# First mixer of a hybrid backbone: gate products on quarters of the TensorE array, and ScalarE in order of issue

## Chip, cores and metric

The kernel runs on one core of one Trainium2 chip. The metric is the device time of one launch in microseconds, as the median of several runs. All inputs start in device memory, laid out by the host in the order in which the kernel loads them; the output is written back there. A core has five engines that matter here: TensorE (PE in the profile; PEld is its weight loads), VectorE (DVE), ScalarE (ACT), GpSimd (POOL) and SyncE (SP), whose queue issues the loads. Each engine takes its instructions one after another, and waits for the others by semaphores.

## The reference, cut to what matters

Two layers work on 256 context tokens and 256 latent tokens of width 1024. Each layer is a SwiGLU feed-forward block, a mixer and a second feed-forward block, with normalisation and modulation around each. The mixer projects to 18 groups of 128 columns, works on them in three families (an RG-LRU on 512 columns, a gated short convolution, a chunked spatial gate) and projects back. The change is about the RG-LRU, for 8 heads of 64 channels and two directions d:

```python
xc = dwconv(p0, lru_conv_w, lru_conv_b, left=2)          # 4 taps, 512 channels
xh = xc.reshape(B, L, 8, 64)
r = sigmoid(einsum('blhi,hij->blhj', xh, w_r[d]) + b_r[d])  # per head: 64 x 64
i = sigmoid(einsum('blhi,hij->blhj', xh, w_i[d]) + b_i[d])
log_a = -8 * r * softplus(-lam[d]);  a = exp(log_a)
bx = sqrt(-expm1(2 * log_a)) * (i * xc)
h = linear_scan(a, bx, h0)                                # h_t = a_t h_(t-1) + bx_t
o_lru = gelu(lru_gate) * (h_forward + h_backward)
```

The second direction runs over the flipped sequence. The latent scan starts from the last state of the context scan. The second layer needs the context only up to its scan states.

## The kernel before, in words

Channels lie on the 128 partitions, tokens on the free axis: context tokens in columns 0 to 255, latent tokens in 256 to 511. A large product is made three times, on the high parts and the low parts of its operands (mm3, col_mm): each weight tile is loaded as `raw`, ScalarE casts it to `hi` and VectorE subtracts to get `lo` (split, L173 and L174), in two halves of 512 columns. `load_split` has four raw buffers and six of hi and lo each. All matmuls pass through one helper, so that they show as line L113.

`mixer(0, ...)` first makes six groups of the input projection (`front`: the four groups of the RG-LRU's input and two of its gates), and then issues the parts named in ORDER[0]. A part is a letter and a number; the engine set in MANUAL, TensorE alone, takes its instructions in exactly this order, while the other engines are ordered by the scheduler. The parts are:

- c, x, b: the three products of the short convolution, 24 products of 512 columns each, with a ScalarE copy (c) or VectorE work behind them
- g, u: a product of 24 and a Gelu on ScalarE; v: four token tiles of 24 products with 256 columns, from two weight units (16 and 17), each holding half of the contraction; m: the spatial mixing, on tiles of 64 columns
- C: the convolution of the RG-LRU for one group c of 128 channels, one ScalarE operation (L701) and three on VectorE (L703)
- G: the gates of a group. Its weights `wbd` are a block diagonal of two heads, 128 x 128, for r and i and both directions, loaded by one DMA of 256 KB (L714). Four products in plain float32 follow, each with a PSUM bank of its own, four sigmoids (L719, L723), and a VectorE product
- D: exp and tanh (L730, L731) and three VectorE operations for each direction
- S: for each direction a root on ScalarE (L741), a VectorE product and the scan (L744, L747, L748), then the sum, the gate, and `put`, which casts the result to high and low parts for the output projection

Weights are fetched ahead in order of use. The function `unit` fills a queue up to three units, and takes the first; a fill issues a unit's DMA and its casts:

```python
def fill(n):
    while units and len(queue) < n:
        queue.append(units.pop(0)())

def unit(ahead=2):
    fill(ahead + 1)
    return queue.pop(0)
```

PSUM has six banks for such products (`pbank`). ScalarE's functions come from tables: a change between sigmoid, exp and tanh, root, and Gelu shows as an ACT_TABLE_LOAD in the trace. After ORDER[0] come the products of the output projection, which need the results 4 to 7 first and 0 to 3 after them. The second layer's mixer has an ORDER of its own; it makes no low parts for its output, and `put` only notes the tile there.

Of the kernel before, what the change touches and what calls it, by code (L numbers as in the profile page):

```python
# [34 lines left out]
PARK = {2: 2, 3: 3, 6: 0, 7: 1}  # L35
NTMP = 3
NSQ = 3
JACC = 'gvg'
FIRST = 2

LAG = ((2.25, 2.1, 1.5), (5.75, 3.75, 1.75))
MANUAL2 = {mybir.EngineType.PE, mybir.EngineType.DVE}
# [3 lines left out]

LATE = ((0,), (1, 2, 3))
MANUAL = {mybir.EngineType.PE}

ORDER = ("c1 C0 g3 G0 C1 C2 C3 D0 c0 x1 G1 G3 D3 x0 S0 D1 v0 S3 G2 b0 g2 D2 u0 m0 S1 b1 u1 m1 S2",  # L50
         "c0 x0 C1 C0 C3 C2 g3 g2 G1 G0 D1 D0 c1 b0 u0 v0 S1 w0 G3 u1 x1 b1 m1 w1 S0 m0 G2 w2 p1 w3 w4 w5 p2 p5 w6 D2 S2 w7 p0 "
         "D3 S3 p7 p4 p3 p6")

TAIL = 4

# [26 lines left out]
def backbone(ctx: ExitStack, tc: tile.TileContext, xT, vecs, crow, w_mod, w_in, w_out, w_mi, w_mo, w_lru, w_cm, b_cm, lam, w_last, out):  # L82
    nc = tc.nc
    ve, sc, gp, te = nc.vector, nc.scalar, nc.gpsimd, nc.tensor
# [3 lines left out]
    tp = ctx.enter_context(tc.tile_pool(name="tp", bufs=2))  # L88
# [7 lines left out]
    def nm(s):  # L96
        cnt[0] += 1
        return f"{s}_{cnt[0]}"

    def tt_(dt=F32, shape=(P, T)):  # L100
        return tp.tile(list(shape), dt, tag="t", name=nm("t"), bufs=NT)

    def pbank():
        return ps.tile([P, 512], F32, tag="mm", name=nm("mm"))
# [23 lines left out]
    pe = Products()  # L128
# [226 lines left out]
    class Norms:  # L355
# [28 lines left out]
        def add(self, s, m):  # L384
# [245 lines left out]
    def mixer(l, segs, nxt, plan, skew_out, order_of, next_unit=None):  # L630

        a0, b0 = SEGS[segs[0]][0], SEGS[segs[-1]][1]
# [8 lines left out]
        for c in range(4):  # L641
            t = tt_(shape=(P, 2, SEQ + 3))
# [54 lines left out]
        def conv(c):  # L697
            xc = tt_()
            o = xc.rearrange("p (s t) -> p s t", s=2)
            cw = lambda k: V("conv_w", (l * 4 + k) * 4 + c)  # L700
            sc.activation(o, xp[c][:, :, 0:SEQ], AF.Identity, scale=cw(0), bias=V("conv_b", l * 4 + c))  # L701
            for k in range(1, 4):
                ve.scalar_tensor_tensor(o, xp[c][:, :, k:k + SEQ], cw(k), o, op0=OP.mult, op1=OP.add)  # L703
            return xc

        xcs, rs, ix, es = {}, {}, {}, {}
        heads = [(c, d, (l * 2 + d) * 4 + c) for c in range(4) for d in range(2)]

        def lru_conv(c):
            xcs[c] = conv(c)  # L710

        def lru_gates(c):
            wbd = tp.tile([P, 4, P], F32, tag="wbd", name=nm("wbd"))
            nc.sync.dma_start(wbd, w_lru[l, c])  # L714
            for c, d, b in heads[2 * c:2 * c + 2]:
                pr = pbank()
                pe.matmul(pr, lhsT=wbd[:, 2 * d, :], rhs=xcs[c], start=True, stop=True)
                r = rs[c, d] = tt_()
                sc.activation(r, pr, AF.Sigmoid, bias=V("b_r", b))  # L719
                pi = pbank()  # L720
                pe.matmul(pi, lhsT=wbd[:, 2 * d + 1, :], rhs=xcs[c], start=True, stop=True)
                i = ix[c, d] = tt_()
                sc.activation(i, pi, AF.Sigmoid, bias=V("b_i", b))  # L723
                ve.tensor_tensor(i, i, xcs[c], op=OP.mult)

        def lru_decay(c):
            for c, d, b in heads[2 * c:2 * c + 2]:
# [7 lines left out]
                ve.tensor_scalar(e, e, -1.0, 1.0, op0=OP.mult, op1=OP.add)  # L735
                es[c, d] = e

        def lru_scan(c):
            for c, d, _ in heads[2 * c:2 * c + 2]:
                e, h, b = es[c, d], rs[c, d], ix[c, d]  # L740
                sc.activation(h, h, AF.Sqrt, scale=-1.0)  # L741
                ve.tensor_tensor(b, b, h, op=OP.mult)
                if d == 0:
                    ve.tensor_tensor_scan(h, e, b, 0.0, op0=OP.mult, op1=OP.add)  # L744
                else:
                    r1, r2 = slice(SEQ - 1, None, -1), slice(T - 1, SEQ - 1, -1)
                    ve.tensor_tensor_scan(h[:, r1], e[:, r1], b[:, r1], 0.0, op0=OP.mult, op1=OP.add)  # L747
                    ve.tensor_tensor_scan(h[:, r2], e[:, r2], b[:, r2], h[:, 0:1], op0=OP.mult, op1=OP.add)  # L748
            h = rs[c, 1]
            ve.tensor_tensor(h[:, a0:b0], h[:, a0:b0], rs[c, 0][:, a0:b0], op=OP.add)  # L750
            ve.tensor_tensor(h[:, a0:b0], h[:, a0:b0], gates[c][:, a0:b0], op=OP.mult)
            put(c, h)

        sc_o, sc_p = {}, {}

# [32 lines left out]
        def chunk_v():  # L788
            wv = [unit(), unit()]
            for tt in range(a0 // P, b0 // P):  # L790
                tok = slice(tt * P, tt * P + P)
                p = pbank()
                mm3(p[:, :256], lambda k: hh[:, k, tok], lambda k: hl[:, k, tok],
                    lambda k: wv[k // 4][0][:, k % 4, :], lambda k: wv[k // 4][1][:, k % 4, :], range(KT))
                if tt % 2 == 0:
                    vt = tt_()
                vs[tt] = vt[:, (tt % 2) * 256:(tt % 2) * 256 + 256]
                sc.activation(vs[tt], p[:, :256], AF.Gelu_apprx_tanh)
# [34 lines left out]
        def out_mm(m, ks):  # L833
            i, o = OUT_AT[m]
            for k in ks:
                first = i not in banks
                if first:
                    banks[i] = pbank()
                pe.matmul(out_bank(m), lhsT=wo[m][:, k, :], rhs=oh[k][:, a0:b0], start=first,
                          stop=(k == LATE[1][-1] and (m + 1 == KT or OUT_AT[m + 1][0] > i)))  # L840

        def out_part(k):
            for m in range(KT):
                out_mm(m, (k,))

        parts = dict(w=out_load, p=lambda m: out_mm(m, (4, 5, 6, 7)), g=gate, c=short_c, x=short_x, b=short_b, v=lambda _: chunk_v(), u=chunk_u, m=chunk_mix,
                     C=lru_conv, G=lru_gates, D=lru_decay, S=lru_scan)
        def issue():
            for part in order_of.split():
                parts[part[0]](int(part[1]))  # L850

        if len(segs) == 2:
            with tc.manual_schedule(engines=MANUAL):
                issue()
            norms = Norms(segs, None, l, 1, nxt)
            order = [4, 5, 6, 7, 0, 1, 2, 3]
            y = norms.y = [tt_() for _ in range(KT)]

            def load(m):
                hi, lo = unit()  # L860
                return (lambda k: hi[:, order[k], :]), (lambda k: lo[:, order[k], :])

            out_phase(range(KT), load, [oh[k] for k in order], [ol[k] for k in order], y, KT,
                      ranges(segs, skew_out), norms.on_y, 0, 1)
            return
# [5 lines left out]
        need(l, 8)  # L871
        need(nxt[0], 3 * nxt[1])
        need(nxt[0], 3 * nxt[1] + 1)
        with tc.manual_schedule(engines=MANUAL):
            issue()
            for k in LATE[0]:
                out_part(k)
        with tc.manual_schedule(engines=MANUAL2):
            pieces = unit_pieces(next_unit)
            yg = [tt_() for _ in range(KT // 2)]  # L880
            acc = [tt_() for _ in range(2)]
# [280 lines left out]
    def keep_up(n):  # L1162

        p = pbank()
        for _ in range(n):
# [5 lines left out]
    ffn(0, 0, both, (0, 1, both), first_units, SKEW)  # L1171

    mixer(0, both, (0, 2, both), staged, SKEW, ORDER[0])
    ffn(0, 1, both, (1, 0, both), staged, SKEW)
    ffn(1, 0, both, (1, 1, both), staged, SKEW, turn=True)
    mixer(1, lat, (1, 2, lat), staged[2:] + staged[:1], 0, ORDER[1],
          lambda j: w_in[1, 1, j])
# [73 lines left out]
```

## Time and profile before

| | |
|---|---|
| median of 3 runs | 1646.99 us (1646.67 to 1647.06) |
| the profiled execution | 1642.21 us, of it 1640.4 us span |
| TensorE busy | 1612.5 us, 98% of the span |
| VectorE, ScalarE, GpSimd busy | 1164.3, 736.7, 120.3 us |
| mean granted clock of TensorE | 0.997 |

The time is that of the launch on the device; the span goes from the first to the last instruction of the profiled execution. An engine's busy time counts the time in which it ran instructions; waiting isn't in it. Matmuls are pipelined, so that one lasts longer in the records than its distance to the next.

### The profile page before, as it was taken

To read this page: it belongs to the slowest core of one execution; us is meant where nothing else is said; L and a number is where in the kernel's file an instruction comes from. 1 tells how busy PE (TensorE), PEld (TensorE's weight loads), DVE (VectorE), ACT (ScalarE), POOL (GpSimd) and SP (SyncE) were. 2 spreads that over 40 slices of the span, in tenths; PEclk is the share of its full clock that TensorE was granted. 3 is DMA by queue.
4 is the path that set the end of the run, shared out by engine and by line. 5 is a ranking of instruction groups with operands and counts; after the bars stand their busy time and mean duration, and the time that the engine had idled before them with its cause. 6 is when DMAs were issued, how large, how long until landed. Compare 5 with 4: busy or idle time off the path is not lost.

```text
span 1640.4 us, 23432 instructions
## 1 busy us (share of the span) xinstructions
PE 1612.5 (98%) x8846; PEld 1371.6 (84%) x8846; DVE 1164.3 (71%) x2183; ACT 736.7 (45%) x1378; POOL 120.3 (7%) x166
## 2 busy tenths in 40 slices
PE   6999999999999999999999999999999999999998
PEld 3788888889977998888888998888888998789997
DVE  4899898548788787867763887767432788785554
ACT  5523322244697662332233462332232479864543
POOL 0000000005000500000000410000000410100000
PEclk9999999999999999999999999999999999999999
DMA  9577677431323225655552215655422316155552
GB/s 370 189 218 261 205 229 223 144 121 44 103 72 120 77 97 187 221 162 174 179 164 80 100 61 194 222 166 167 141 90 90 103 54 210 47 167 194 180 191 78
DMA packets 73906, 249.97 MB, mean 152 GB/s; under 512 B 8384, under 2 KB 10048, under 8 KB 73792
## 3 DMA queue, kind: packets, MB, share of 16 engines
q1 hardware_dynamic: 73216, 247.94, 45.9%
q8 instruction: 69, 1.13, 0.3%
q10 hardware_dynamic: 576, 0.52, 0.1%
q14 instruction: 45, 0.37, 0.1%
HBM read 247.39 MB, written 1.05 MB: 151 GB/s over the span
## 4 chain that ended last, share of the span: by engine, by line
PE 89%; DVE 6%; ACT 3%; DMA 1%; issue 1%; POOL 0%; SPq 0%; POOLq 0%; DVEq 0%; ACTq 0%
PE mm L113 87%; PE st L113 1%; DVE x L271 1%; DVE sq L394 1%; DVE t L703 0%; PE mod L113 0%; DVE z L270 0%; DVE tmp L262 0%; DMA x<-in_xT 0%; ACT hi L173 0%; DVE t L397 0%; POOL rs L241 0%; DVE t L332 0%; DMA raw<-in_w_mi 0%; ACT t L730 0%
## 5 line engine op out<-in xcount | busy, mean ns | idle before, releaser
L173 ACT CAST hi<-raw 128x512 fp32r<-128x512 f32 (+1 forms) x596 | 343.6, 610 | 672.7 <-PE mm L113 475.8
L113 PE MATMUL mm<-hh,hi 128*128 128x512 f32 (+1 forms) x1840 | 625.6, 348 | 0.5 <-ACT hh L1095 0.2
L113 PE MATMUL mm<-hl,hi 128*128 128x512 f32 (+1 forms) x1840 | 622.5, 346 | 1.8 <-DVE hl L256 1.0
L174 DVE TENSOR_TENSOR lo<-raw,hi 128x512 fp32r<-128x512 f32 (+1 forms) x596 | 387.5, 680 | 157.3 <-ACT hi L173 154.5
L113 PE MATMUL mm<-hh,lo 128*128 128x512 f32 (+1 forms) x1840 | 466.6, 346 | 0.0
L113 PEld LDWEIGHTS mm<-hh,hi 128*128 128x128 f32 x1840 | 345.5, 188 | 52.1 <-ACT hh L1095 2.8
L113 PEld LDWEIGHTS mm<-hl,hi 128*128 128x128 f32 x1840 | 345.9, 188 | 51.2 <-DVE hl L1101 1.6
L113 PEld LDWEIGHTS mm<-hh,lo 128*128 128x128 f32 x1840 | 325.1, 188 | 47.2
L196 DVE SCALAR_TENSOR_TENSOR junk<-raw,cb 128x1024 bf16<-128x1024 f32 x256 | 312.9, 1222 | 70.8 <-DMA raw<-in_w_mod 67.1
L113 PE MATMUL mm<-t,hi 128*128 128x512 f32 (+1 forms) x1056 | 240.6, 367 | 0.0
L113 PEld LDWEIGHTS mm<-t,hi 128*128 128x128 f32 x1056 | 182.8, 188 | 35.7 <-issue 0.2
L397 POOL TENSOR_TENSOR t<-t,sq 128x256 f32<-128x256 f32 x112 | 94.2, 856 | 712.2 <-ACT sq L391 702.3
L113 PE MATMUL mm<-t,lo 128*128 128x512 f32 (+1 forms) x528 | 131.5, 367 | 0.0
L113 PEld LDWEIGHTS mm<-t,lo 128*128 128x128 f32 x528 | 92.6, 188 | 17.7
L480 DVE TENSOR_TENSOR sg<-sg,mm 128x512 f32<-128x512 f32 (+1 forms) x72 | 45.9, 640 | 78.3 <-PE mm L113 78.3
L113 PE MATMUL mm<-t,hh 128*128 128x256 f32 x512 | 71.2, 281 | 0.0
L113 PEld LDWEIGHTS mm<-t,hh 128*128 128x128 f32 x512 | 65.7, 188 | 0.5
L173 ACT CAST t<-sg 128x512 fp32r<-128x512 f32 (+1 forms) x94 | 50.6, 541 | 32.0 <-DVE sg L480 29.0
L332 DVE TENSOR_TENSOR t<-t,mm 128x256 f32<-128x256 f32 (+1 forms) x66 | 35.4, 536 | 29.3 <-PE mm L113 29.1
L174 DVE TENSOR_TENSOR t<-sg,t 128x512 fp32r<-128x512 f32 (+1 forms) x94 | 55.3, 589 | 0.9 <-ACT t L173 0.9
L113 PE MATMUL mm<-hi,t 128*128 128x512 f32 x176 | 55.1, 394 | 0.0
L263 ACT ACTIVATE hh<-tmp,modv 128x256 fp32r<-128x256 f32 x72 | 42.4, 596 | 22.1 <-DVE tmp L262 21.9
(179 smaller groups left out, 1212.4 us busy)
## 6 DMA issues: line engine op xcount, KB each, us to landing
raw<-in_w_in SPq DMA_DIRECT2D x176, 512.0 KB, 3.6
raw<-in_w_mod SPq DMA_DIRECT2D x128, 512.0 KB, 4.3
raw<-in_w_out SPq DMA_DIRECT2D x48, 512.0 KB, 3.3
raw<-in_w_mi SPq DMA_DIRECT2D x36, 512.0 KB, 4.1
raw<-in_w_last SPq DMA_DIRECT2D x22, 512.0 KB, 3.3
raw<-in_w_out SPq DMA_DIRECT2D x24, 384.0 KB, 3.7
t<-in_w_mod SPq DMA_DIRECT2D x32, 256.0 KB, 5.8
raw<-in_w_mo SPq DMA_DIRECT2D x8, 512.0 KB, 3.7
```

The costliest lines, as they stand in the source:

```text
L113: te.matmul(dst, lhsT=lhsT, rhs=rhs, start=start, stop=stop)
L173: sc.copy(hi, src)
L174: ve.tensor_tensor(lo, src, hi.bitcast(F32), op=OP.subtract)
L196: ve.scalar_tensor_tensor(junk, raw.rearrange("p k c -> p (k c)"), 1.0, cb[:, s], op0=OP.mult, op1=OP.mult, accum_out=modv[l][:, v, m, s:s ...
L263: sc.activation(hh[:, m, a:b], tmp, AF.Identity, scale=A, bias=B)
L271: ve.scalar_tensor_tensor(x[:, m, a:b], z, mcol(l, 3 * i + 2, m, s), x[:, m, a:b], op0=OP.mult, op1=OP.add)
L332: ve.tensor_tensor(y[m][:, a:b], y[m][:, a:b], p[:, :b - a], op=OP.add)
L394: ve.scalar_tensor_tensor(q[2], y, G, x[:, m, a:b], op0=OP.mult, op1=OP.mult)
L397: (gp if JACC[c] == "g" else ve).tensor_tensor(acc[c], acc[c], q[c], op=OP.add)
L480: ve.tensor_tensor(sg[:, :b - a], sg[:, :b - a], pu[:, :b - a], op=OP.mult)
```

## The change

In the first layer's mixer (QUARTERS = (0,)):

- The gate weights are loaded without the zeros, 64 x 64 per head, gate and direction, by four DMAs in place of one. After a convolution, `lru_swap` copies its result into a second tile with the two heads exchanged, by two DMAs from POOL's queue. A gate product on the whole array becomes two on quarters: r takes the rows 0 to 63 and i the rows 64 to 127, each with its two heads in the two halves of the columns. Where a head doesn't lie in the rows of its gate, it is taken from the swapped tile. r and i go to two different banks.
- ScalarE joins TensorE in the set whose instructions are taken in order of issue.
- The roots (R), the scans (S) and the casts of the results (H) are parts of their own, and `l` fills the queue of weights to a number. ORDER[0] is another order of all these; ORDER[1] writes R, S, H where S stood.

The second layer keeps whole gate products; its gate weights take the pool tag of the swapped tiles.

```diff
+QUARTERS = (0,)
 MANUAL = {mybir.EngineType.PE}
-ORDER = ("c1 C0 g3 G0 C1 C2 C3 D0 c0 x1 G1 G3 D3 x0 S0 D1 v0 S3 G2 b0 g2 D2 u0 m0 S1 b1 u1 m1 S2",
+IN_ORDER = {mybir.EngineType.PE, mybir.EngineType.Activation}
+ORDER = ("c1 C0 C1 g3 C2 C3 G0 G1 l4 D0 D1 x1 c0 R0 R1 S0 S1 G3 x0 G2 D3 D2 H0 H1 R3 R2 b0 S3 v0 g2 S2 H3 u0 m0 b1 H2 u1 "
+         "m1",
...
         def lru_conv(c):
             xcs[c] = conv(c)
+            if l in QUARTERS:
+                lru_swap(c)
+        turned_xc = {}
+        def lru_swap(c):
+            t = turned_xc[c] = tp.tile([P, T], F32, tag="swap", name=nm("swap"), bufs=2)
+            for a, b in ((0, P // 2), (P // 2, 0)):
+                gp.dma_start(t[a:a + P // 2], xcs[c][b:b + P // 2])
+        def gate_products(c):
+            if l in QUARTERS:
+                wbd = tp.tile([P, 2, 2, P // 2], F32, tag="wbd", name=nm("wbd"))
+                for g in range(2):
+                    for h in range(2):
+                        a = 64 * h
+                        src = w_lru[l, c].rearrange("p (d g) o -> p d g o", g=2)
+                        nc.sync.dma_start(wbd[64 * g:64 * g + 64, :, h], src[a:a + 64, :, g, a:a + 64])
+            else:
+                wbd = tp.tile([P, 4, P], F32, tag="swap", name=nm("wbd"))
+                nc.sync.dma_start(wbd, w_lru[l, c])
+            def products(d):
+                ps2 = pbank(), pbank()
+                for g, p in enumerate(ps2):
+                    if l not in QUARTERS:
+                        pe.matmul(p, lhsT=wbd[:, 2 * d + g, :], rhs=xcs[c], start=True, stop=True)
+                        continue
+                    for h in range(2):
+                        src = (xcs if g == h else turned_xc)[c]
+                        rows, cols = slice(64 * g, 64 * g + 64), slice(64 * h, 64 * h + 64)
+                        pe.matmul(p[cols], lhsT=wbd[rows, d, h], rhs=src[rows], start=True, stop=True)
+                return ps2
+            return products
...
-                pr = pbank()
-                pe.matmul(pr, lhsT=wbd[:, 2 * d, :], rhs=xcs[c], start=True, stop=True)
+                pr, pi = products(d)
                 r = rs[c, d] = tt_()
                 sc.activation(r, pr, AF.Sigmoid, bias=V("b_r", b))
-                pi = pbank()
-                pe.matmul(pi, lhsT=wbd[:, 2 * d + 1, :], rhs=xcs[c], start=True, stop=True)
...
+        def lru_root(c):
+            for d in range(2):
+                sc.activation(rs[c, d], rs[c, d], AF.Sqrt, scale=-1.0)
         def lru_scan(c):
-                sc.activation(h, h, AF.Sqrt, scale=-1.0)
...
-            put(c, h)
+        def lru_put(c):
+            put(c, rs[c, 1])
...
-                     C=lru_conv, G=lru_gates, D=lru_decay, S=lru_scan)
+                     C=lru_conv, G=lru_gates, D=lru_decay, R=lru_root, S=lru_scan, H=lru_put, l=fill)
...
-            with tc.manual_schedule(engines=MANUAL):
+            with tc.manual_schedule(engines=IN_ORDER if l in QUARTERS else MANUAL):
                 issue()
```

## Rows read from the trace of the kernel before

**Rows 1.** The page: busy time by engine, and lines of the chain.

```profile
PE 1612.5 (98%) x8846; PEld 1371.6 (84%) x8846; DVE 1164.3 (71%) x2183; ACT 736.7 (45%) x1378; POOL 120.3 (7%) x166
PE mm L113 87%; PE st L113 1%; DVE x L271 1%; DVE sq L394 1%; DVE t L703 0%; PE mod L113 0%; DVE z L270 0%; DVE tmp L262 0%; DMA x<-in_xT 0%; ACT hi L173 0%; DVE t L397 0%; POOL rs L241 0%; DVE t L332 0%; DMA raw<-in_w_mi 0%; ACT t L730 0%
```

**Rows 2.** First mixer by stage: stretch, length, busy by engine, clock, DMA, GB/s.

```profile
441.60:456.20 14.60, 14.60 (x59) 10.54 (x57) 7.53 (x11) 8.30 (x15) 0.00 (x0) 1.00 0.60 192
456.20:474.30 18.10, 18.10 (x66) 12.06 (x65) 16.82 (x30) 17.99 (x27) 0.00 (x0) 1.00 0.19 58
474.30:491.20 16.90, 16.90 (x122) 15.82 (x121) 16.83 (x32) 16.74 (x23) 0.00 (x0) 1.00 0.25 79
491.20:511.40 20.20, 20.20 (x81) 14.75 (x79) 17.32 (x30) 17.39 (x28) 0.00 (x0) 1.00 0.35 117
511.40:524.90 13.50, 13.50 (x82) 10.69 (x81) 13.40 (x24) 10.35 (x15) 0.00 (x0) 1.00 0.12 42
```

**Rows 3.** TensorE's timeline at G0: start, length, instruction, shape, count.

```profile
450.47 1.80 PE L113 MATMUL mm<-hh,lo 128*128 128x512 f32 x7
...
452.80 3.59 PE L113 MATMUL mm<-t,wbd 128*128 128x512 f32 x8
...
453.66 0.19 PEld L113 LDWEIGHTS mm<-t,wbd 128*128 128x128 f32 x1 [0.24 <-issue]
...
454.09 0.19 PEld L113 LDWEIGHTS mm<-t,wbd 128*128 128x128 f32 x1 [0.24 <-issue]
```

**Rows 4.** TensorE's timeline at the start: 32-column tiles, first idle time.

```profile
14.38 1.87 PE L113 MATMUL st<-ones,t 128*128 128x2 f32 x8 [14.38 <-DVE t L1063]
16.18 1.93 PE L113 MATMUL mod<-t,cs 128*32 128x512 f32 x8
...
22.79 2.09 PE L113 MATMUL mod<-t,cs 128*32 128x512 f32 x16
```

**Rows 5.** TensorE's timeline at m0: into 64-column tiles and out.

```profile
511.08 0.40 PE L113 MATMUL mm<-hh,lo 128*128 128x512 f32 x1
511.41 1.09 PE L113 MATMUL mm<-wcm,t 128*64 128x128 f32 x16
...
512.77 0.40 PE L113 MATMUL mm<-hl,hi 128*128 128x512 f32 x1
```

**Rows 6.** ScalarE's timeline behind G0 and at D0.

```profile
454.41 1.28 ACT L719 ACT_TABLE_LOAD   x1
455.70 0.69 ACT L719 ACTIVATE t<-mm,vec 128x512 f32<-128x512 f32 x1
456.29 0.68 ACT L723 ACTIVATE t<-mm,vec 128x512 f32<-128x512 f32 x1
...
461.55 1.34 ACT L730 ACTIVATE t<-t,s 128x512 f32<-128x512 f32 x2
...
464.02 0.56 ACT L759 COPY t<-mm 128x512 f32<-128x512 f32 x1
464.49 0.62 ACT L173 CAST hi<-raw 128x512 fp32r<-128x512 f32 x1
```

**Rows 7.** VectorE: one timeline row, and a line group of the mixer's stretch.

```profile
458.86 4.77 DVE L703 SCALAR_TENSOR_TENSOR t<-t,vec,t 128x512 f32<-128x512 f32 x7
...
L744 DVE TENSOR_TENSOR_SCAN t<-t,t 128x512 f32<-128x512 f32 x4 | 4.9, 1219 | 0.0
```

**Rows 8.** DMA issues by line with time to landing; SP's issues of wbd.

```profile
out<-t SPq DMA_DIRECT2D x4, 128.0 KB, 1.8
...
L714 SPq DMA_DIRECT2D wbd<-in_w_lru x8: 327/328/424, 21.2 to 1369.6; - x8
...
DMA to landing us min/median/max: 2.6/3.5/6.9
```

**Rows 9.** ScalarE's line groups of 441.6 to 524.9 us: busy, mean ns.

```profile
L741 ACT ACT_TABLE_LOAD x5 | 6.4, 1283 | 0.1
...
L741 ACT ACTIVATE t<-t 128x512 f32<-128x512 f32 x8 | 4.8, 629 | 0.1
```

More of the change, by code (lines that the diff above doesn't have):

```diff
@@ L48 @@
 MANUAL = {mybir.EngineType.PE}
-ORDER = ("c1 C0 g3 G0 C1 C2 C3 D0 c0 x1 G1 G3 D3 x0 S0 D1 v0 S3 G2 b0 g2 D2 u0 m0 S1 b1 u1 m1 S2",
-         "c0 x0 C1 C0 C3 C2 g3 g2 G1 G0 D1 D0 c1 b0 u0 v0 S1 w0 G3 u1 x1 b1 m1 w1 S0 m0 G2 w2 p1 w3 w4 w5 p2 p5 w6 D2 S2 w7 p0 "
-         "D3 S3 p7 p4 p3 p6")
+IN_ORDER = {mybir.EngineType.PE, mybir.EngineType.Activation}
+ORDER = ("c1 C0 C1 g3 C2 C3 G0 G1 l4 D0 D1 x1 c0 R0 R1 S0 S1 G3 x0 G2 D3 D2 H0 H1 R3 R2 b0 S3 v0 g2 S2 H3 u0 m0 b1 H2 u1 "
+         "m1",
+         "c0 x0 C1 C0 C3 C2 g3 g2 G1 G0 D1 D0 c1 b0 u0 v0 R1 S1 H1 w0 G3 u1 x1 b1 m1 w1 R0 S0 H0 m0 G2 w2 p1 w3 w4 w5 p2 "
+         "p5 w6 D2 R2 S2 H2 w7 p0 D3 R3 S3 H3 p7 p4 p3 p6")
 TAIL = 4
@@ L710, in lru_conv @@
             xcs[c] = conv(c)
+            if l in QUARTERS:
[28 more added lines that the diff above has]
+            return products
         def lru_gates(c):
-            wbd = tp.tile([P, 4, P], F32, tag="wbd", name=nm("wbd"))
-            nc.sync.dma_start(wbd, w_lru[l, c])
+            products = gate_products(c)
             for c, d, b in heads[2 * c:2 * c + 2]:
-                pr = pbank()
-                pe.matmul(pr, lhsT=wbd[:, 2 * d, :], rhs=xcs[c], start=True, stop=True)
+                pr, pi = products(d)
                 r = rs[c, d] = tt_()
                 sc.activation(r, pr, AF.Sigmoid, bias=V("b_r", b))
-                pi = pbank()
-                pe.matmul(pi, lhsT=wbd[:, 2 * d + 1, :], rhs=xcs[c], start=True, stop=True)
                 i = ix[c, d] = tt_()
@@ L736, in lru_decay @@
                 es[c, d] = e
+        def lru_root(c):
+            for d in range(2):
+                sc.activation(rs[c, d], rs[c, d], AF.Sqrt, scale=-1.0)
         def lru_scan(c):
-            for c, d, _ in heads[2 * c:2 * c + 2]:
+            for d in range(2):
                 e, h, b = es[c, d], rs[c, d], ix[c, d]
-                sc.activation(h, h, AF.Sqrt, scale=-1.0)
                 ve.tensor_tensor(b, b, h, op=OP.mult)
@@ L873, in mixer @@
         need(nxt[0], 3 * nxt[1] + 1)
-        with tc.manual_schedule(engines=MANUAL):
+        with tc.manual_schedule(engines=IN_ORDER if l in QUARTERS else MANUAL):
             issue()
@@ L877, in mixer @@
                 out_part(k)
-        with tc.manual_schedule(engines=MANUAL2):
+        with tc.manual_schedule(engines=MANUAL2 | IN_ORDER if l in QUARTERS else MANUAL2):
             pieces = unit_pieces(next_unit)
```

## The prediction

> **What bounds the kernel now.** I read the page first, then the stretch of the first mixer by stages, then the three queues that meet in it. The page: TensorE is busy 98% of the span, and the chain that ended last is 87% matmuls of one helper line [rows 1]. So a part off TensorE counts only where TensorE ends up waiting for it. The stages from 441.6 to 524.9 us are what ORDER[0] issues: TensorE is busy in every microsecond, with no idle at all, while VectorE and ScalarE are nearly as full from 456 to 511 us (16.8 and 18.0 of 18.1 us in one stage) and POOL does nothing [rows 2]. There is thus a stall to lose here and none to win: a change gains by shortening TensorE's own work, and loses by any wait that it puts into that order, which is written out by hand. A part of 24 products (c, g, x, b, u) takes 24 x 0.233 = 5.6 us: seven products take 1.80 us with a last one of 0.40 [rows 3].
>
> **The gates.** One G part is eight passes that start 0.43 us apart, 3.43 us in all [rows 3]; four parts are 13.7 us. After the change four quarter products stand where two whole ones stood. What quarters do together no row shows. The nearest are the four-column tiles at the start: sixteen passes in 2.09 us [rows 4], where one after another they would take 16 x 0.43 = 6.9. If quarters overlap as well, a G part is four steps of 0.43, 1.72 us. Going into tiles and out costs about 0.4 us: the mixing products with two tiles begin at 511.41 after a product that began at 511.08, and the second product behind them begins at 512.77 [rows 5], 1.2 us for what is 0.86 at the pace within them. With G0 and G1 adjacent there are three such trips. Sum: 4 x 1.72 + 3 x 0.4 = 8.1 us, a gain of 5.6 us. The other end: if row halves take turns, 3.43 a part and a loss of 1.2; if all take turns, 6.9 a part and a loss of 15. I take the gain, nearest to rows 4.
>
> The Trainium skill, "TensorEngine Tiling (Array Packing)", section "PSUM Bottleneck", warns that after tiling the emptying of PSUM may become the bound. Here the rows bear on it directly: four sigmoids follow each other at 0.58 us [rows 6], 2.3 us against 2.0 for a tiled part (8.1 over 4), so by that rule the gain would be 5.6 - 4 x 0.3 = 4.4 us, and the whole 1.2 us worse.
>
> **The beginning.** TensorE runs c1 and g3 until 452.8, then G0 and G1 back to back. G0 now needs C0's swapped copy. C0's first operation follows c1's copy on ScalarE (447.2, where c1 ends, + 0.5 + 0.2 + 0.72, so near 449); its three VectorE operations at 0.67 [rows 7] and a subtraction between them end by 451.8. A POOL-issued copy inside SBUF is in no row; the ends are 1.8 us (128 KB stores from SBUF) and 6.9 (the slowest wbd load) [rows 8]. I take 2.5, the store plus issue, so G0 starts at 454.4. Nothing queues behind it on POOL. The Trainium skill, "DMA: Bandwidth & Descriptors", section "Anatomy of one DMA — SWDGE (gpsimd) path", gives about 2.0 us plus bytes over 436 GB/s, an estimate of 2.3 us for one half; by it the sum stays.
> The copy isn't last, though. ScalarE, now in order, does g3's Gelu (from 453.0), the first operations of C2 and C3 (0.5 + 2 x 0.72, to 455.1) and a table load of 1.28 before the first sigmoid [rows 6], at 456.4. Eight gate banks in a row don't fit into six; G1's last pair waits for two sigmoids (457.6), runs 0.86, and x1 starts at 458.7 with the trip out. Without waits it were 456.6. Cost: 2 us. With the slowest copy it is 4 us more.
>
> **The weight casts in order.** This is the term that decides. ScalarE now takes casts of weights in the place where a part asks for them, two units ahead. The casts of unit 17, the second half of v0's weights, are issued at the head of b0, behind R2. v0 needs them after eight products (0.12 us each, an estimate: half the columns of rows 3). Between c0's end and that cast ScalarE's list is: a copy 0.5; loads for sqrt, sigmoid, exp, sqrt, 4 x 1.28 = 5.1; eight roots at 0.6, 4.8 [rows 9]; eight sigmoids at 0.58, 4.6; eight exp or tanh at 0.62, 5.0 [rows 6]; five casts at 0.5, 2.6. That is 22.6 us, and 0.6 for the VectorE subtraction and 0.3 for a semaphore's way: 23.5. TensorE has between the same points G3, x0, G2, b0 and the eight products: 2.15 + 5.6 + 2.15 + 5.6 + 0.95 = 16.4 us. So TensorE, which can't pass v0, stands still for 7 us at least, from 486.3 (458.7 + 11.2 for x1, c0 + 16.4).
> VectorE makes it longer. R2's roots need D2's products, and H1's cast needs S1. Counted in order of issue from 449, VectorE has before R2: 12 convolution operations at 0.67; 40 others of 512 columns at 0.63 (8 subtractions, 8 for gates, 16 for decays, 8 around the scans); 4.9 for the scans of two parts [rows 7]; some 8.5 of short ones (an estimate of half an operation each, in the decays and in x1 and x0): 46.5 us. With 2 us in which it waits for C2 and C3 it ends at 497.5; root, cast and subtraction bring 499, a stall of 12.6. VectorE isn't bound to the order of issue, and x0's and G2's operations (4 us) may fall behind. Between 7 and 12.6 I take 10.
> In before, unit 17 had no such place: ScalarE's order was free. The ten table loads that go (17 in six such lines, five of them the roots' [rows 9], become 7, at 1.28 us), 12.8 us of ScalarE, are worth nothing by themselves: they are late where they count, before v0, and plenty after it.
>
> **The clock.** Before its first matmul TensorE was idle 14.4 us; eight passes then took 1.93 us, as long as sixteen (2.09) from 22.8 us on [rows 4]: by their pace the 1.2 GHz level, then 2.4. A 10 us stall should bring the same; some 4 us of work at half pace cost 2 us (0 if the level holds, 3 by the whole stretch from 14.4 to 20).
>
> **What costs nothing.** SP issues wbd in four pieces, 0.33 us each [rows 8]; those hoisted to 21 and 45 us delay other loads by 1 us, hidden while TensorE works on loaded tiles, at worst +1. The second mixer gets the same instructions, roots a step earlier; its ScalarE stays free: 0, give or take 1. After v0 ScalarE and VectorE have room, and the output products find H1 to H3 ready; but since TensorE was never idle there, nothing is won back.
>
> **Sum.** -5.6 + 2 + 10 + 2 = +8.4 us. The profiled span is 1640.4 (the execution 1642.2, runs 1647.0, 4.8 above it): 1648.8 for a span, 1655.4 for the median.
>
> **Rivals.**
> *Casts in time (other side, faster).* If unit 17's casts stand ahead of R2 on ScalarE (its order not as strict as I read, or VectorE and ScalarE a good 7 us quicker), v0 doesn't wait and -5.6 + 2 = -3.6 remains, 1643.4; with no wait at G0 1641.4. It decides where the cast lands before 486.3. For it: ScalarE drops ten loads. Against it: the 22.6 us are a plain sum of one queue. Chance 0.26, of which 0.07 is within 0.2%.
> *Quarters don't overlap.* Row halves in turn add 1.7 us a part; G3 and G2 hide behind v0's stall, G0 and G1 don't: +8.4 + 3.4 = 11.8, 1658.8. No row shows row tiles. 0.06.
> *A slow copy.* With 6.9 us for the swap everything shifts 4: 1659.4. It can be no more than that for C2 and C3, needed ten microseconds later. 0.05.
> *Gain and stall cancel.* A v0 wait of 5 with no fall of the clock: -5.6 + 2 + 5 = +1.4, 1648.4. 0.05.
> *Forecast.* 0.58, its own range 1650 to 1661.5 (stall 7 without the clock's cost, to 12.6 with 3), 0.04 of it within 0.2%.
>
> Within 0.2% (3.3 us) is what a measurement of this kernel can't tell from no change. Faster 0.19 rounds to 0.20, the same 0.15, slower 0.65. The range goes from 1642.5, which leaves out the best of the first rival, to 1661.5.
>
> **What would show it.** Gates: G parts of about 2 us in place of 3.43, quarter passes starting together. Beginning: TensorE idle 1.5 to 3 us ahead of G0, sigmoids from 456.4. Casts: ScalarE's last roots directly ahead of two casts, near 493 to 498 us, TensorE idle up to then after the eighth product of v0, then at half clock. Wrong is the prediction if TensorE passes v0 without a gap, if ScalarE's casts overtake roots, or if quarter passes start 0.43 us apart.

## The result, and the profile after

The changed kernel takes 1660.09 us (median of 4 runs, 1659.58 to 1660.60) against 1646.83 for the kernel before (1646.65 to 1647.06): 13.3 us more, ratio 1.008 with a 95% interval of 1.0063 to 1.0098. The forecast, slower by 8.4 us, had the direction right and the time inside the range, but 4.7 us too low.

The profiled executions lie 18.4 us apart (spans 1658.8 and 1640.4), since that of before was some 4.6 us below its kernel's median and that of the changed kernel 0.5 above. The page after, as in [rows 1]:

```profile
PE 1616.6 (97%) x8878; PEld 1374.7 (83%) x8878; DVE 1166.2 (70%) x2183; ACT 724.4 (44%) x1368; POOL 125.0 (8%) x174
...
PE mm L117 87%; PE st L117 1%; DVE x L275 1%; DVE sq L398 1%; PE mod L117 0%; DMA wo<-in_w_mo 0%; DVE z L274 0%; DVE t L783 0%; DVE tmp L266 0%; DMA x<-in_xT 0%; DVE t L785 0%; DVE t L401 0%; DVE t L772 0%; DVE t L770 0%; POOL rs L245 0%
```

The chain now has `DVE t L783` and `L785`, a VectorE product and a scan of the mixer, which it hadn't before: TensorE waits for VectorE somewhere in there. The windows of the first mixer say where (stretch, length, busy time and instructions of PE, PEld, DVE, ACT and POOL, clock, DMA share, GB/s; the stages are c1 with g3, G0 with G1, x1 to b0, v0, and g2 to m1, of which the last has no idle time either):

```profile
443.08:454.37 11.29, 11.29 (x51) 8.84 (x49) 4.16 (x7) 3.70 (x7) 0.41 (x1) 1.00 0.19 60
454.37:462.75 8.38, 6.41 (x34) 1.77 (x33) 6.46 (x10) 6.97 (x11) 2.86 (x6) 1.00 0.66 174
462.75:489.40 26.65, 26.65 (x131) 19.01 (x129) 24.41 (x44) 24.97 (x37) 1.03 (x2) 1.00 0.25 74
489.40:517.48 28.08, 13.72 (x98) 13.18 (x96) 25.91 (x46) 13.80 (x23) 0.00 (x0) 0.76 0.23 75
517.48:542.21 24.73, 24.73 (x130) 19.47 (x128) 12.67 (x20) 11.11 (x21) 0.00 (x0) 1.00 0.26 87
```

The mixer takes 99.1 us where it took 83.3 (441.6 to 524.9 in [rows 2]). TensorE has idle time in two stages: 2 us in G0 and G1, and 14.4 us in v0, which takes 28.1 us where it took 11.2. Of the other 2.5 us of difference between the spans 1.5 lie ahead of the mixer and 1.0 behind it; in both places this execution has a stretch at half clock that before's hadn't, or had for half as long (413.5 to 416.9 us, and 13.6 us from 1454.6 against 6.7 us from 1437.5). TensorE's timeline shows both waits:

```profile
454.37 1.07 PE L117 MATMUL mm<-t,wbd 64*64 64x512 f32 x2
456.37 1.24 PE L117 MATMUL mm<-swap,wbd 64*64 64x512 f32 x3 [0.93 <-DMA swap<-t]
...
460.88 0.61 PE L117 MATMUL mm<-swap,wbd 64*64 64x512 f32 x1 [1.04 <-ACT t L759]
...
474.14 0.64 PE L117 MATMUL mm<-t,wbd 64*64 64x512 f32 x1
474.15 0.65 PE L117 MATMUL mm<-swap,wbd 64*64 64x512 f32 x2
...
476.02 0.50 PE L117 MATMUL mm<-hh,hi 128*128 128x512 f32 x1
...
490.32 0.28 PE L117 MATMUL mm<-lo,hh 128*128 128x256 f32 x1
500.73 0.58 PE L117 MATMUL mm<-hi,hh 128*128 128x256 f32 x1 [10.13 <-ACT hi L177]
505.54 0.58 PE L117 MATMUL mm<-lo,hh 128*128 128x256 f32 x1 [4.23 <-DVE lo L178]
```

G3, which waits for nothing, takes 1.88 us to the next product (474.14 to 476.02). Its quarter passes start 10 ns apart, where the passes of [rows 3] start 0.43 us apart. So quarters in different rows do run together. A whole part takes 3.03 us to the next product (h2, below), and that product's successor starts 0.63 us behind it, in place of 0.34 behind quarters: a part on quarters is 1.4 us shorter, where the prediction has 5.6 for four.

In v0 TensorE does eight products and stands until ScalarE's first cast of unit 17, does one more, and stands again until VectorE's subtraction. From start to start less one product's 0.12 us these are 10.3 and 4.7 us, 15.0 together. ScalarE's and VectorE's timelines show why:

```profile
495.86 1.23 ACT L778 ACTIVATE t<-t 128x512 f32<-128x512 f32 x2 [1.21 <-DVE t L772]
498.94 1.23 ACT L778 ACTIVATE t<-t 128x512 f32<-128x512 f32 x2 [1.85 <-DVE t L772]
500.08 1.12 ACT L177 CAST hi<-raw 128x512 fp32r<-128x512 f32 x2
```

```profile
500.10 0.68 DVE L178 TENSOR_TENSOR t<-t,t 128x512 fp32r<-128x512 f32 x1
500.70 0.68 DVE L826 TENSOR_TENSOR t<-t,mm 128x512 f32<-128x512 f32 x1
...
501.90 1.28 DVE L783 TENSOR_TENSOR t<-t,t 128x512 f32<-128x512 f32 x2
...
504.24 0.66 DVE L788 TENSOR_TENSOR_SCAN t<-t,t 128x256 f32<-128x256 f32 x1
504.82 1.26 DVE L178 TENSOR_TENSOR lo<-raw,hi 128x512 fp32r<-128x512 f32 x2
```

Unit 17's casts come directly behind the last roots, which wait for VectorE twice. Both casts are done by 501.2, but VectorE subtracts only at 504.82: the low parts of a result, b0's product and the first operations of S3 come first. While TensorE stands, the granted clock falls to half (the 1.2 GHz level), and rises again only after 3.5 us of products:

```profile
490.44:500.73 10.29, 0.16 (x2) 0.00 (x0) 10.29 (x23) 7.19 (x12) 0.00 (x0) 0.74 0.16 51
500.73:505.54 4.81, 0.58 (x1) 0.29 (x2) 4.81 (x9) 4.45 (x7) 0.00 (x0) 0.50 0.00 0
505.54:509.06 3.52, 3.52 (x16) 3.52 (x17) 3.52 (x6) 0.00 (x0) 0.00 (x0) 0.50 0.44 150
```

The wait in G1 is named after ScalarE (`ACT t L759`), but ScalarE isn't its cause. Views of the copies by time of issue, first C0's first half, then C1's two halves, with their times to landing:

```profile
L724 POOL DMA_DIRECT2D swap<-t x1: 696/696/696, 454.0 to 454.0; - x1
...
DMA to landing us min/median/max: 2.4/2.4/2.4
```

```profile
L724 POOL DMA_DIRECT2D swap<-t x2: 523/523/523, 455.2 to 455.7; - x2
...
DMA to landing us min/median/max: 3.6/4.3/5.1
```

C1's second half was issued at 455.7 and landed 5.1 us later, at 460.8, when TensorE goes on. The PSUM banks were free by then: six banks go round, so that G1's last two products take those that G0's first two sigmoids empty, and these two ended at 458.5 and 459.05.

```profile
457.79 0.69 ACT L759 ACTIVATE t<-mm,vec 128x512 f32<-128x512 f32 x1
458.37 0.68 ACT L761 ACTIVATE t<-mm,vec 128x512 f32<-128x512 f32 x1
```

Two other runs with G0 and G1 side by side show the same (below).

### The profile page after: what moved, and what is told of

It reads as the page before. It is cut to its first block, busy times and chain, and to the rows that moved or that the text cites. A ratio compares the mean times of both kernels' runs of the same rounds, so it can differ in the third digit from the quotient of the medians.

```text
span 1658.8 us, 23535 instructions
## 1 busy us (share of the span) xinstructions
PE 1616.6 (97%) x8878; PEld 1374.7 (83%) x8878; DVE 1166.2 (70%) x2183; ACT 724.4 (44%) x1368; POOL 125.0 (8%) x174
## 4 chain that ended last, share of the span: by engine, by line
PE 89%; DVE 7%; ACT 2%; DMA 1%; issue 1%; POOL 0%; SPq 0%; POOLq 0%; DVEq 0%
PE mm L117 87%; PE st L117 1%; DVE x L275 1%; DVE sq L398 1%; PE mod L117 0%; DMA wo<-in_w_mo 0%; DVE z L274 0%; DVE t L783 0%; DVE tmp L266 0%; DMA x<-in_xT 0%; DVE t L785 0%; DVE t L401 0%; DVE t L772 0%; DVE t L770 0%; POOL rs L245 0%
```

## The experiments

In each table and text, "mixer" is the time from c1's first product to the first product behind the last part. Ratios are to the kernel before on the same chip, with 95% intervals. The kernel before varied between 1640.8 and 1649.2 us over these runs, and the intervals reach 0.1 to 0.2% to either side. The expectations give the theories as they were held then.

| run | mixer, us | median, us | ratio |
|---|---|---|---|
| before | 83.3 | | |
| changed kernel | 99.1 | 1660.09 | 1.0080 (1.0063 to 1.0098) |
| e1, casts ahead of D3 | 88.7 | 1648.57 | 1.0024 (1.0015 to 1.0033) |
| e2, ScalarE free | 81.9 | 1645.00 | 1.0003 (0.9993 to 1.0013) |
| e3, quarters in the old order | 85.1 | 1646.03 | 1.0010 (0.9999 to 1.0021) |
| e4, new order, whole gates | 98.2 | 1658.14 | 1.0086 (1.0070 to 1.0101) |
| f1, C3 ahead of C2 | 81.3 | 1644.77 | 0.9999 (0.9986 to 1.0012) |
| f2, G0 later | 92.3 | 1652.19 | 1.0047 (1.0031 to 1.0063) |
| f3, l4 ahead of x0 | 86.8 | 1648.03 | 1.0021 (1.0011 to 1.0032) |
| f4, the same, c0 ahead of G0 | 88.0 | 1648.70 | 1.0027 (1.0015 to 1.0038) |
| g1, C0 and C1 first | 79.8 | 1642.24 | 0.9986 (0.9977 to 0.9995) |
| g2, the same, x0 and g2 moved | 83.8 | 1642.71 | 0.9987 (0.9976 to 0.9997) |
| h1, g1 with g2 last | 79.9 | 1641.38 | 0.9986 (0.9976 to 0.9996) |
| h2, h1 with whole gates | 83.3 | 1644.91 | 1.0004 (0.9993 to 1.0016) |

### What the loss is: e1, e2, e3, e4

e1 fills the weight queue ahead of D3, so that unit 17's casts precede the eight exp and tanh and the four roots:

```diff
-G3 x0 G2 D3 D2 H0 H1 R3 R2 b0
+G3 x0 G2 l3 D3 D2 H0 H1 R3 R2 b0
```

> Theory A (the casts of unit 17 stand behind R2 on ScalarE, and v0 waits for them and for the subtraction): one part l3 ahead of D3 puts these casts some 7 us earlier in ScalarE's order and ahead of the decays in VectorE's, the 15 us wait in v0 shrinks to 0 to 8, and the half clock behind it goes: 1645 to 1653 us. Theory B (the quarter gates with their copies and waits cost the time): the first half of the mixer stays as it is, 1658 to 1661 us. Theory C (ScalarE in order loses the same wherever a cast stands, since it is the full engine): the wait moves behind v0, 1656 to 1660 us.

One part in the order takes 10.5 us off the mixer, as theory A has it; B and C asked for 1656 us or more. The wait for the cast is gone; one for the subtraction is left, which VectorE again does behind x0's and G2's operations, as TensorE's and VectorE's timelines show:

```profile
492.54 0.58 PE L117 MATMUL mm<-lo,hh 128*128 128x256 f32 x1 [3.96 <-DVE lo L178]
```

```profile
491.81 1.28 DVE L178 TENSOR_TENSOR lo<-raw,hi 128x512 fp32r<-128x512 f32 x2
```

e2 takes ScalarE out of the set that follows the order:

```diff
-IN_ORDER = {mybir.EngineType.PE, mybir.EngineType.Activation}
+IN_ORDER = {mybir.EngineType.PE}
```

> Same parts and same order for TensorE, ScalarE's order free again. Theory A: weight casts overtake the roots, no wait in v0, the gates' gain of about 5 us less the start's wait of 2 to 3 us shows: 1642 to 1646 us. Theory B: the waits stay with the gates, 1655 us or more.

v0 takes 11.2 us, as in before, and the time is within theory A's range. TensorE's only waits are those of G0 and G1, and one of 1.5 us in the output product, for a cast. Its windows, of G0 with G1 and of the rest of the mixer:

```profile
451.97:459.93 7.96, 6.41 (x34) 1.64 (x33) 7.35 (x12) 7.88 (x13) 3.15 (x6) 1.00 0.56 163
459.93:522.52 62.59, 62.59 (x355) 49.68 (x353) 57.31 (x101) 44.14 (x73) 1.03 (x2) 1.00 0.30 94
```

e3 makes the quarters alone: ScalarE free, and the parts of before in their order, with R, S and H where S stood.

```diff
+ORDER = ("c1 C0 g3 G0 C1 C2 C3 D0 c0 x1 G1 G3 D3 x0 R0 S0 H0 D1 v0 R3 S3 H3 G2 b0 g2 D2 u0 m0 R1 S1 H1 b1 u1 m1 R2 S2 H2",
```

> Quarter gates alone, in the order of before, ScalarE free. Theory A: the four G parts take 2.0 us in place of 3.43 (5.6 us less), G0 stands directly behind g3 and waits some 3 us for its copy: 1643 to 1645 us. Theory B: 1650 us or more.

The mixer becomes 1.8 us longer than in before, and the kernel no faster. G0 takes 4.11 us and G1 with G3 8.95, where a part without a wait takes 1.88 (G2 in this run). The time fits neither theory: it lies 1 us above A's range, and 4 below B's.

e4 is the changed kernel with whole gate products and without the copies:

```diff
-QUARTERS = (0,)
+QUARTERS = ()
...
-            with tc.manual_schedule(engines=IN_ORDER if l in QUARTERS else MANUAL):
+            with tc.manual_schedule(engines=IN_ORDER if l in (0,) else MANUAL):
```

> ScalarE in order and the new order alone, with whole gate products. Theory A: the time at which unit 17's casts come is set by ScalarE and VectorE, so the longer gates of G3 and G2 hide in the wait of v0, and the whole is within 3 us of the change: 1657 to 1663 us. Theory B: without quarters the loss goes, 1645 to 1650 us.

It loses as much as the change, without a single quarter, and in the same place, as theory A has it:

```profile
497.00 0.58 PE L117 MATMUL mm<-hi,hh 128*128 128x256 f32 x1 [7.30 <-ACT hi L177]
...
501.82 0.58 PE L117 MATMUL mm<-lo,hh 128*128 128x256 f32 x1 [4.23 <-DVE lo L178]
```

So the loss is the place of unit 17 in ScalarE's list, and VectorE's behind it: moving it (e1), freeing ScalarE's order (e2) and leaving out the quarters (e4) agree. What stays open after these four is why the quarters win nothing where ScalarE is free.

### Where the gates' gain goes: f1, f2

In e3 TensorE stood 2.6 us between G1 and G3. POOL issued C3's copy only when G1 had given its buffer back, since the swapped tiles have two buffers; POOL's timeline and then TensorE's:

```profile
468.47 1.03 POOL L723 DMA_DIRECT2D swap<-t  x2 [6.02 <-DVE t L818]
```

```profile
470.99 1.59 PE L116 MATMUL mm<-swap,wbd 64*64 64x512 f32 x3 [2.01 <-DMA swap<-t]
```

The releaser that is named for POOL is again the last event, not the cause: G1's last pass on the swapped tile began at 467.54, 0.9 us earlier, and 0.9 us lie as well between G1's last pass (462.19) and such an issue (463.08) in the changed kernel, where the profile names TensorE. f1 exchanges two convolutions, so that C3's copy takes the buffer of G0.

```diff
-c1 C0 g3 G0 C1 C2 C3 D0 c0 x1 G1 G3
+c1 C0 g3 G0 C1 C3 C2 D0 c0 x1 G1 G3
```

> Quarters alone in the order of before, ScalarE free, as in the third run, but the convolution of group 3 is issued ahead of that of group 2, so that group 3's swapped copy takes the buffer that G0 gives back and not the one that G1 holds. In the third run TensorE stood 2.60 us between G1 and G3 for that copy and ran the rest of G3 at half pace. Theory C (the gates' 5.6 us are eaten by the swapped copies: 2.1 us at G0, 5.0 at G1 and G3): G1 and G3 together take 4.5 to 6 us in place of 8.95, the G0 wait stays at 1.2 us, and the time falls by 3 to 4 us, to 0.997 to 0.999 of the kernel before. Rival D (the gain goes elsewhere, to VectorE and ScalarE, which are as full as before): TensorE waits in x0 or v0 instead and the ratio stays at 1.000 to 1.002.

G1 with G3 takes 5.17 us in place of 8.95, and the mixer 81.3 us in place of 85.1, as theory C has it. The time doesn't show it (ratio 0.9999, where theory C had 0.997 to 0.999): the output products, which start earlier, now wait for m1's result to be cast.

```profile
529.62 0.73 PE L116 MATMUL mm<-t,hi 128*128 128x512 f32 x2 [1.53 <-ACT t L176]
```

f2 lets G0 start later, behind all convolutions and c0:

```diff
-c1 C0 g3 G0 C1 C3 C2 D0 c0 x1 G1 G3
+c1 C0 C1 g3 C3 C2 c0 G0 D0 x1 G1 G3
```

> As the run before, with C1 ahead of g3 and all convolutions and c0 ahead of G0, so that G0 starts 5.6 us later and finds its swapped copy. Theory C: all four G parts run at 2.0 us with at most 0.5 us of waiting, the first mixer ends 4 to 6 us earlier than in before, the ratio is 0.996 to 0.998. Rival D: ScalarE and VectorE, which start on the gates 5.6 us later, bring a wait of 3 us or more in x0 to v0, and the ratio stays at 0.999 to 1.001.

G0 takes 1.88 us, but theory C's time is missed by far. Rival D has the cause, ScalarE that starts later, but neither the place nor the size: the ratio is 1.0047, above its range, and the waits are not in x0 to v0. G1 with G3 takes 7.64 us, waiting for sigmoids, and G2 9.29, since its banks are held by v0's Gelus:

```profile
499.70 1.11 PE L116 MATMUL mm<-t,wbd 64*64 64x512 f32 x1 [6.02 <-ACT t L840]
```

### ScalarE in order, with the casts earlier: f3, f4

```diff
-R0 R1 S0 S1 G3 x0 G2 D3 D2
+R0 R1 S0 S1 G3 l4 x0 G2 D3 D2
```

> The changed kernel with one more fill of the weight queue, l4 between G3 and x0, so that unit 17's casts and subtractions are issued ahead of x0, G2, D3 and D2. With l3 ahead of D3 a wait of 4.2 us in v0 was left, for the subtraction on VectorE. Theory A (all of the loss in v0 is the place of unit 17 in ScalarE's and VectorE's lists): no wait in v0 over 0.5 us, no half clock behind it, 15 to 17 us less than the changed kernel, ratio to before 0.998 to 1.000 (the gates' 5.6 us less some 3.6 us of waiting at G0 and G1). Rival E (ScalarE in order is itself too late for v0, whatever is cast first): the wait moves to v0's first products or to b0 and stays at 3 us or more, ratio 1.002 or more.

v0 loses no more than 0.4 us, in pieces, so that theory A is right about v0. But g2 behind it waits 2.8 us, since its unit's casts stand behind the same roots. Rival E has the ratio (1.0021) and the cause, though not the place.

```profile
502.24 0.79 PE L116 MATMUL mm<-hh,hi 128*128 128x512 f32 x1 [2.67 <-ACT hi L176]
```

f4 has c0 ahead of G0 as well (`C2 C3 c0 G0 G1 l4 D0 D1 x1`).

> As the run before, with c0 moved ahead of G0, so that the swapped copy has landed and ScalarE has done its table load when G0 starts. Theory A with C: G0 and G1 take 5 to 6 us in place of 8.2 (the two waits for PSUM banks stay, 1 to 2 us), no wait in v0, ratio to before 0.996 to 0.999. Rival E: what G0 gains is given back in v0, since sigmoids, exps and roots start 3 us later on ScalarE: ratio 1.000 or more.

All copies of C0 and C1 have landed soon after G0 starts at 457.55 (C1's second half at 458.2), and G0 with G1 takes 4.33 us in place of 8.1 to 8.4. This with eight gate banks in a row: so the wait at G1 in the changed kernel was the copy, and not PSUM, as some of these expectations and the prediction say. The banks do cost something once the copies are there: the 0.6 us over twice 1.88 are the last two products, which go on at 460.31 and 460.88, 0.06 us behind the ends of the first two sigmoids. What is won is given back at G2 (1.55 and 0.68 us) and g2 (1.50 and 0.65), and the ratio is rival E's.

### A version that waits for no copy: g1, g2, h1, h2

The inputs of C0 and C1 are there before c1 starts, and POOL and VectorE have room. g1 issues them first:

```diff
-c1 C0 g3 G0 C1 C3 C2 D0 c0 x1 G1 G3
+C0 C1 c1 g3 G0 C3 C2 D0 c0 x1 G1 G3
```

> The run with group 3's convolution first, and now C0 and C1 ahead of c1, whose inputs are there before c1 starts, so that C0's swapped copy has landed when G0 starts. In the two runs before with quarters and ScalarE free TensorE lost 2.2 us at G0 to the copy, 1.4 at G1 and G3 to sigmoids that hold the banks, and then 1.6 to 2.2 in the first output products, which wait for m1's result to be cast. Theory C (the gates' 5.6 us go into these three waits): G0 takes 1.9 to 2.2 us in place of 4.1, the first mixer from c1 to m1 takes 79 to 80 us in place of 81.3 (83.3 in before), and the output products wait 2 us or more, so that the ratio is 0.998 to 1.000. Rival F (the mixer is bound by VectorE and ScalarE, so that any time won at the head comes back as a wait before v0): 81 us or more from c1 to m1.

G0 takes 1.88 us and the mixer 79.8, both as theory C has it, and the kernel is faster than before, by 0.05 to 0.23%. The output products still wait, 1.3 and 0.4 us, a little less than theory C's 2 us.

g2 puts x0 between G1 and G3, and g2 behind m1:

```diff
-G1 G3 D3 x0 R0 S0 H0 D1 v0 R3 S3 H3 G2 b0 g2 D2 u0 m0 R1 S1 H1 b1 u1 m1 R2 S2 H2
+G1 x0 G3 D3 R0 S0 H0 D1 v0 R3 S3 H3 G2 b0 D2 u0 m0 R1 S1 H1 b1 u1 m1 g2 R2 S2 H2
```

> As the run before, with x0 between G1 and G3, so that ScalarE has given G1's banks back, and g2, whose result is needed only for the last four results of the output product, behind m1, so that m1's cast has 5.6 us of cover. Theory C: all four G parts at 1.9 to 2.2 us, no wait over 0.5 us from c1 to the output products, 78.0 to 79.0 us from c1 to the end of the last part (83.3 in before), ratio 0.996 to 0.998. Rival F: a wait of 2 us or more in v0, G2 or b0, and ratio 0.999 or more.

The wait of the output is gone, but G2 comes directly behind v0 with no product between, and waits for its Gelus, at half clock. By its trace rival F is right (83.8 us in the mixer), and theory C is not; the time is that of g1.

```profile
492.59 1.11 PE L116 MATMUL mm<-t,wbd 64*64 64x512 f32 x1 [2.62 <-ACT t L840]
```

h1 is g1 with g2 alone behind m1, and h2 the same with whole gate products and no copies:

> The run with C0 and C1 first, with g2 moved from b0's side to behind m1, and G1 and G3 left side by side. Theory C: G2 finds its banks as in that run (x0 and b0 stay where they were), the wait of 1.3 and 0.4 us in the first output products goes, and from c1 to the end of the last part it takes 79 to 80.5 us: ratio 0.9970 to 0.9985. Rival F (VectorE and ScalarE bound the stretch): with 5.6 us less of TensorE work between v0 and m1 a new wait of 1.5 us or more comes up in b0, u0 or m0, and the ratio stays at 0.9985 to 1.000.

> The same order as the run before with whole gate products and no swapped copy, ScalarE free: what the quarters alone are worth, where nothing waits for the copy. Theory C: the four G parts take 3.0 to 3.4 us each, 12.5 us together, against 9.1 to 9.5 with quarters (two with 1.9, one pair with 5.2 to 5.9 for the banks); TensorE works from c1 to the last part without a gap, and the time is 3 to 5 us above the run before, ratio 0.999 to 1.001. Rival F: the time is within 1.5 us of the run before, since VectorE and ScalarE, and not the gates' passes, set the end.

The windows of h1 and then of h2 (G0; G1 with G3; the rest to g2's end):

```profile
454.28:456.16 1.88, 1.88 (x17) 0.51 (x16) 1.04 (x2) 1.86 (x4) 0.00 (x0) 1.00 0.24 98
...
467.56:473.43 5.87, 5.10 (x34) 1.40 (x33) 5.87 (x13) 5.83 (x11) 1.02 (x2) 1.00 0.51 156
473.43:522.84 49.41, 49.41 (x291) 40.49 (x290) 47.55 (x82) 43.76 (x63) 0.00 (x0) 1.00 0.22 70
```

```profile
453.87:456.90 3.03, 3.03 (x10) 1.35 (x8) 1.38 (x2) 3.00 (x5) 0.00 (x0) 1.00 0.06 24
...
468.49:474.95 6.46, 6.46 (x17) 2.87 (x16) 6.46 (x14) 6.26 (x10) 0.00 (x0) 1.00 0.37 122
474.95:526.01 51.06, 51.06 (x282) 41.49 (x281) 48.03 (x82) 44.28 (x64) 0.00 (x0) 1.00 0.28 89
```

h2 has no gap, and neither gains nor loses against before. h1 is 3.5 us shorter in the mixer, and 3.5 us shorter by the medians, as h2's theory C has it; the two intervals overlap by a little (0.9993 to 0.9996), and rival F, a difference of less than 1.5 us, is out by the mixers. Of h1's own theory the mixer is right and the output is not: its products still wait (1.49 us in one place), and the interval doesn't set h1 apart from g1.

Between them the two runs say what the quarters are worth in this order: 3.5 us. Four times 1.4 would be 5.6; G1 and G3 side by side take 2.1 us more than twice 1.88, and all of it goes by PSUM banks. G3's second product starts at 470.0, when VectorE has read x1's bank (until 469.90), and its third and fourth at 471.85 and 472.42, behind the first two sigmoids, which start only after a table load and end at 471.80 and 472.37. TensorE's and ScalarE's timelines:

```profile
471.85 0.64 PE L116 MATMUL mm<-t,wbd 64*64 64x512 f32 x1 [0.77 <-ACT t L758]
```

```profile
471.11 0.69 ACT L758 ACTIVATE t<-mm,vec 128x512 f32<-128x512 f32 x1
471.69 0.68 ACT L760 ACTIVATE t<-mm,vec 128x512 f32<-128x512 f32 x1
```

This is the rule of the Trainium skill, "TensorEngine Tiling (Array Packing)", section "PSUM Bottleneck", that the emptying of PSUM may become the bound once the products are packed. Here the trace agrees, at 1.36 us from one pass to the next (470.49 to 471.85), in that one place.

## Why the prediction came out right, and where it was too low

**The gates** (predicted -5.6): right, in the mechanism and in the size. From G0 to v0 the new order takes 36.1 us with whole products (e4, 452.49 to 488.60) and 35.0 with quarters (454.37 to 489.40), a gain of 1.1, in which G0 and G1 take 8.38 us. Had they taken 4.33, as in f4, or 3.76, as two parts of 1.88, the gain were 5.1 or 5.7.

**The beginning** (predicted +2): the first half of the mechanism was right, the second and the size were not. By the same numbers G0 and G1 waited 4.1 to 4.6 us. The copy of C0 landed 2.4 us after issue, where 2.5 was taken. The step that failed is the next one, that G1 waits for two sigmoids: it waited for C1's second copy, which took 5.1 us, longer than those sigmoids. So x1 began at 462.75, where the prediction's 458.7 and the 1.5 us by which this mixer started later give 460.2. By the landing events of the trace that copy was there at 460.79 us in the changed kernel, at 458.67 in e1 and 459.22 in f3, and TensorE went on 0.06 to 0.09 us later each time, while the sigmoid that the profile names is not the same (r's in the changed kernel, i's in e1 and f3). The Trainium skill, "DMA: Bandwidth & Descriptors", section "Anatomy of one DMA — SWDGE (gpsimd) path", led to an estimate of 2.3 us; the first two copies agree with it (2.4 and 2.3), the third and fourth do not (3.6 and 5.1). The prediction had 6.9 us as the far end and tried it on the whole chain, not on the later copies alone.

**The casts in order** (predicted +10, bounds 7 and 12.6): the mechanism was right, and this is the term that was mis-sized most, at 15.0. The prediction's walk through VectorE ends at 497.5, with the same 1.5 us at 499.0, and the last roots began at 498.94: nothing fell behind there, though the choice of 10 in place of 12.6 counted on it. Wrong was then "root, cast and subtraction bring 499": the subtraction was taken as following its cast at once. VectorE had 4.2 us of other work first, and that stood beyond the upper bound too. So TensorE went on at 505.5 and not at 500.5; it had also come 2.6 us later (490.4 in place of 487.8), which took as much off the stall. In e1 the same happened once more: the cast in time, the subtraction 4.2 us late. The 0.3 us for a semaphore's way is a term that no run shows: TensorE went on 0.05 to 0.09 us behind the event that it waited for (h1, f4 and the landings above).

**The clock** (predicted +2): v0 took 28.08 us, of which 11.2 are work and 15.0 waiting; the other 1.9 are the products at half pace.

**Sum.** -1.1 for gates and beginning, +15.0, +1.9: 15.8, and the mixer became 15.9 longer. The forecast for these terms was 8.4. That the time came out 4.7 us above the forecast, and not 7.5 or, with the 2.5 us ahead of the mixer and behind it, 10, is luck: the prediction took the 6.6 us between span and median of before for the changed kernel as well, where only 1.3 lie between them. What makes that distance is not settled; the section on the hardware shows the likeliest part of it. The upper end of the range is no better founded: the terms named for it (a stall of 12.6, 3 for the clock) add up to +12.0 and 1659.0 us, not 1661.5, and the measured 1660.09 lies above that sum.

**The rivals.** "Casts in time" would have been right with ScalarE free: e2 has no wait in v0. It then still has no gain that can be measured: G0 and G1 take 7.96 us against 4.33 without the late copies, and 1.5 us go to the output product, 5.1 together. "Gain and stall cancel" is out by the 15 us in v0. "Quarters don't overlap" is out by G3's 1.88 us. "A slow copy" is true of C1's.

**What costs nothing**: no wait of TensorE is for the small weight loads, and copies that ran beside these alone took 2.4 to 2.5 us (e1, e3, f1, f2); all that lies behind the first mixer, the second one with it, differs by the 1.0 us named above. The ten table loads that went won nothing that can be measured: e2 is without them too.

## What to carry to other kernels

An engine that is put in order takes everything along that is issued on it, prefetches too: follow each prefetched weight through both engines that prepare it, and place the fill by the slower of them. Time won on a bounding engine is kept only if what it then waits for moves forward as well: 5.6 us in the gates were worth nothing that can be measured until the convolutions were issued early enough for their copies to land (g1, h1). And where a named releaser ended at the moment at which a DMA landed, look at the same wait in other runs: the name changed between them, the landing did not.

## What the runs showed of the hardware that was not expected

Four copies of 128 KB inside SBUF, issued by POOL within 1.7 us, landed 2.4, 2.3, 3.6 and 5.1 us after issue in the changed kernel. In f1 the four copies of C3 and C2, issued as closely, took 2.2 to 2.7; in f2 the two of C3, alone on POOL's queue, took 4.9 and 5.6. So it isn't the number of copies. Views of the DMA traffic while they were under way, of the changed kernel (455 to 461 us) and of f1 (463 to 468 us):

```profile
swap<-t POOLq DMA_DIRECT2D x5, 128.0 KB, 2.4
raw<-in_w_mi SPq DMA_DIRECT2D x1, 512.0 KB, 5.2
wbd<-in_w_lru SPq DMA_DIRECT2D x4, 32.0 KB, 2.8
```

```profile
swap<-t POOLq DMA_DIRECT2D x4, 128.0 KB, 2.4
```

Where copies were slow, a large load of weights ran beside them (in f2 the DMA engines were busy for 0.81 of the time); where they ran alone, they weren't. In all runs with quarters every copy that took more than 2.75 us had a load of 512 KB under way before it landed; with nothing beside them, or the loads of 32 KB alone, they took 2.2 to 2.7. In the changed kernel, e1, f3, f4, g1, g2 and h1 such a load was issued between the third and the fourth copy: the first two took 2.3 to 2.4 us, the third 3.4 to 3.7 and the fourth 4.9 to 5.3. That is read from the issue and landing times of these runs; no run moved that load alone.

Short stretches at the 1.2 GHz level come and go between executions without any difference in what the kernel does there. In the execution of [rows 1] the mean clock was 0.997, and its only such stretch inside its work was one of 6.7 us near 1437. The execution of g2 has one there too, of 6.7 us, and more elsewhere, at 414, 957, 1332 and 1452; two of its windows at half clock, of which the second is its wait at G2:

```profile
413.80:417.20 3.40, 3.40 (x17) 3.40 (x18) 2.71 (x9) 1.18 (x3) 0.71 (x1) 0.50 0.45 153
492.30:499.10 6.80, 6.51 (x18) 4.04 (x19) 4.90 (x9) 6.09 (x12) 0.00 (x0) 0.50 0.14 39
```

Each stretch of 3.4 us at half pace costs about 1.7 us. Their number differs from execution to execution, and the time goes with it: over the 104 runs of the kernel before that the experiments have, on four chips, the correlation of the time with the mean granted clock is -0.85 to -0.91 on each chip (-1 would be a straight line). The 42 runs at 0.997 took 1640.8 to 1644.2 us, the 7 at 0.992 took 1648.1 to 1649.2. So most of the spread of 8 us between runs of one kernel goes with the clock, and so, likely, do most of the 5.4 us by which this execution of g2 (1648.16 us, clock 0.991) was above its median. What sets off these stretches was not measured.
